# The rotation of queries and keys on GpSimd, issued behind VectorE's scalings in a hybrid attention kernel

## The chip, the cores and the metric

The kernel runs on one core of one Trainium2 chip. The metric is the device time of one execution in microseconds; lower is better. The core has five engines that run their own instruction queues and wait for one another through semaphores: TensorE (PE, with its weight loads as PEld), VectorE (DVE), ScalarE (ACT), GpSimd (POOL) and SyncE (SP, which only issues DMAs here).

## The reference

One layer of a decoder on a prompt of 2048 tokens and a sample batch of 8 x 8 tokens, all in float32, width 1024. One input projection feeds two groups of heads: group A, attention in a window of 128 positions with rotary positions, 8 query heads, 2 key heads and a learned sink per head; group B, gated linear attention. Both go through one output projection, then an MLP of width 4096. The change concerns group A alone:

```python
def rope(x, pos):
    ...
    x1, x2 = xf[..., :half], xf[..., half:]
    return jnp.concatenate([x1 * cos - x2 * sin, x2 * cos + x1 * sin], axis=-1).astype(x.dtype)

def sink_softmax(scores, mask, sink):
    scores = jnp.where(mask, scores, -jnp.inf)
    m = jnp.maximum(jnp.max(scores, axis=-1, keepdims=True), sink)
    p = jnp.exp(scores - m)
    return p / (jnp.sum(p, axis=-1, keepdims=True) + jnp.exp(sink - m))
```

In `swa_banded` each block of 128 queries sees its own and the previous block of keys: scores, `sink_softmax`, product with the values.

## The kernel before

The tokens are cut into 17 tiles: 16 of 128 prompt tokens and one of the 64 sample tokens. The program runs in stages: attention of group A (to about 345 us of the profile), then group B with the output projection, then the MLP. Within the attention stage one pass of the loop `for i in range(NB)` is a block: it computes attention for tile `i` and, between, the projection (`proj`), rotation and transposes for the tiles after it.

A block has four units, one per key head `r` and pair of query heads `jj`, in the order (0,0), (0,1), (1,0), (1,1). `unit` is a generator; each `next` issues one step: a copy of the sinks by GpSimd (L466), scores on TensorE (`sc`), masking and maximum on VectorE (into `s` and `m`), the exponential on ScalarE (which also sums into `den`), the division (a reciprocal of `den` and two scalings of `s` by it on VectorE), transposes on TensorE (`pT`), copies into a high part `ph` (ScalarE) and a low part `pl` (VectorE), products with the values on TensorE (`av`), and the sum `mo`. In loop step `u` the current unit `now` goes through mask to transposes, the unit `behind` finishes and the unit `ahead` starts. So each step `u` has one pair of scalings.

The order on TensorE, ScalarE and VectorE is written by hand: the wrapper `InOrder` (`te`, `ac`, `dv`) chains the instructions, and L141 is its line, so almost all of these engines' rows carry L141. GpSimd's order isn't chained; a scheduler places its instructions in the one queue by when it expects their inputs. The small jobs beside the units (`todo`) are placed by `A_PLAN`: a name, a step `u`, and a phase of it (A, X, B or C, in this order). `"turn": "1A"` is the rotation of tile `i + 1`.

`rotate` makes five GpSimd instructions: two products with the sine into `tb` (L385), one product with the cosine in place in `qk` (L391), and two additions into `rot` (L394, L400). TensorE transposes `rot` into `pq` and `pk` in step 2 of a block (`heads_T`), from which the operands `qh`, `ql`, `kh`, `kl` are made; GpSimd copies halves of the last two (L432, L436, L437, L443). In 8 blocks GpSimd also prepares weights of group B: two products with the gains (L271) and two subtractions (L273, `wg`), and in some blocks VectorE copies constants (L855).

Of the kernel before, what the change touches and what calls it, by code (L numbers as in the profile page):

```python
# [55 lines left out]
A_FILL = ((11, 2, 0), (10, 0, 2), (10, 0, 0), (12, 1, 0))  # L56
A_LEAD, A_SPLIT, A_PL_FIRST = 14, (2, 0, 0, 0), ()
A_PLAN = [(name, (int(at[0]), at[1])) for name, at in dict(
    first="1B", hi1="3B", x1="1B", lo1="0A", x0="0C", rest="3A", lo0="3A", junk="2A", turn="1A", rstd="1A", vl="3B"
).items()]  # L60
G_FIRST = (0, 1)
G_NEXT = (NB, *range(2, NB))
# [64 lines left out]
def f32(ap):  # L127
    return ap.bitcast(F32)
# [23 lines left out]
def hybrid_step_kernel(ctx: ExitStack, tc: tile.TileContext, I, O):  # L152
    nc = tc.nc
# [11 lines left out]
    def rows(i):  # L165
        return min(P, NTOK - i * P)
# [12 lines left out]
    def bank(shape, kind, name):  # L179

        return ps.tile(shape, F32, tag=kind, name=name, bufs=1 if kind in "de" else 2)
# [102 lines left out]
    sp = open_pool("a_s")  # L284
    sp.tile([P, 8], F32, name="a_edge")
    gxTs, ropes, xs_in, xTs, proj, qks, rots, heads, vals = {}, {}, {}, {}, {}, {}, {}, {}, {}
    stores = []

    stages = [("cache_k", 1), ("cache_v", 1), ("s", 3), ("ph", 2), ("pl", 2), ("qh", 2), ("ql", 2), ("mo", 2), ("tb", 1)]
    stages = [t for t in stages for _ in range(t[1])]  # L290
# [56 lines left out]
    def scaled(out, i, src):  # L347
        ac.activation(out, src, AF.Copy, scale=rstd_all[: rows(i), i : i + 1])

    def take_first(i):  # L350

        n = rows(i)
        qks[i] = sp.tile([P, 10, HD], F32, tag="qk", name=f"qk_{i}", bufs=2)
        scaled(qks[i].rearrange("p h d -> p (h d)")[:n, :A_N], i, proj.pop((i, 0))[:n, :A_N])

    def take_rest(i):

        n = rows(i)
        p_ = proj.pop((i, 1))
        w = 640 - A_N  # L360
        scaled(qks[i].rearrange("p h d -> p (h d)")[:n, A_N:640], i, p_[:n, :w])
        vps = p_[:n, w:A_N]
        if i == NB:
            vals[i] = vn = sp.tile([NS, P], F32, tag="vv", name="vn", bufs=4)
            scaled(vn, i, vps)
            return lambda: None
        vals[i] = vv = sp.tile([P, 2, 2, HD], F32R, tag="vv", name=f"vv_{i}", bufs=4)
        vh, vl = vv[:, :, 0, :], vv[:, :, 1, :]
        vps = vps.rearrange("p (r d) -> p r d", r=2)
        scaled(vh, i, vps)  # L370
        if i == NB - 1:
            vo = sp.tile([P, P], F32, tag="kc", name="vo", bufs=1)
            scaled(vo, i, p_[:n, w:A_N])
            stores.append((O["v_win_prompt"][0, 0].rearrange("w h d -> w (h d)"), vo))
        rs = rstd_all[:n, i : i + 1]
        return lambda: dv.scalar_tensor_tensor(vl, vps, rs, f32(vh), op0=ALU.mult, op1=ALU.subtract)

    def rotate(i, engine=nc.gpsimd):

        n = rows(i)  # L380
        qk, rope = qks.pop(i), ropes.pop(i)
        tb = sp.tile([P, 10, HD], F32, tag="tb", name=f"tb_{i}", bufs=1)
        for hf in range(2):
            sin = rope[:n, 1, hf * 32 : hf * 32 + 32].unsqueeze(1).to_broadcast([n, 10, 32])
            engine.tensor_tensor(  # L385
                tb[:n, :, hf * 32 : hf * 32 + 32], qk[:n, :, 32 - hf * 32 : 64 - hf * 32], sin, op=ALU.mult
            )
            if hf == 0:
                yield
        cos = rope[:n, 0, :].unsqueeze(1).to_broadcast([n, 10, HD])  # L390
        engine.tensor_tensor(qk[:n], qk[:n], cos, op=ALU.mult)  # L391
        yield
        rots[i] = rot = sp.tile([P, 5, 2, HD], F32, tag="rot", name=f"rot_{i}", bufs=1)
        engine.tensor_tensor(  # L394
            rot[:n, 0:4].rearrange("p j r d -> p r j d"),
            qk[:n, 0:8].rearrange("p (r j) d -> p r j d", r=2),
            tb[:n, 0:8].rearrange("p (r j) d -> p r j d", r=2),
            op=ALU.add,
        )
        engine.tensor_tensor(rot[:n, 4], qk[:n, 8:10], tb[:n, 8:10], op=ALU.add)  # L400
        yield
# [56 lines left out]
    def unit(i, r, jj, mo):  # L458

        nkt = min(i + 1, 2)  # L460
        nk = nkt * P
        rr = half_of[r]
        u_ = f"{i}_{r}_{jj}"
        h0 = r * 4 + jj * 2
        s = sp.tile([P, 2, nk + 1], F32, tag="s", name=f"s_{u_}", bufs=3)
        nc.gpsimd.tensor_copy(s[:, :, nk : nk + 1], sink[:, h0 : h0 + 2].unsqueeze(2))  # L466
        yield
        qs, ks, kl = heads[i]
        kh, kl = (t[:, r].rearrange("p a k -> p (a k)")[:, 2 * P - nk :] for t in (ks, kl))
        sc = bank([P, 2, nk], "b", f"sc_{u_}")  # L470
        for u in range(2):
            j = jj * 2 + u
            te.matmul(sc[:, u, :], qs[r][:, j, :], kh, start=True, stop=False)
            te.matmul(sc[:, u, :], qs[r][:, j, :], kl, start=False, stop=True)
        yield
        m = sp.tile([P, 2], F32, tag="m", name=f"m_{u_}", bufs=3)
        for u in range(2):
            dv.tensor_tensor_reduce(
                s[:, u, :nk], sc[:, u, :], amask[:, 2 * P - nk :], scale=1.0,
                scalar=sink[:, h0 + u : h0 + u + 1], op0=ALU.add, op1=ALU.min, accum_out=m[:, u : u + 1],  # L480
            )
        yield
        den = sp.tile([P, 2], F32, tag="den", name=f"den_{u_}", bufs=3)
        for u in range(2):
            ac.activation(
                s[:, u, :], s[:, u, :], AF.Exp, scale=-1.0, bias=m[:, u : u + 1], accum_out=den[:, u : u + 1]
            )
        yield
        dv.reciprocal(den, den)
        for u in range(2):  # L490
            dv.tensor_scalar(s[:, u, :nk], s[:, u, :nk], den[:, u : u + 1], None, op0=ALU.mult)
        yield
        pT = bank([P, nkt, 2, P], "c", f"pT_{u_}")
        for u in range(2):
            for kt in range(nkt):
                te.transpose(pT[:, kt, u, :], s[:, u, kt * P : (kt + 1) * P], ident)
        yield
        ph = sp.tile([P, nkt, 2 * P], F32R, tag="ph", name=f"ph_{u_}", bufs=2)
        pl = sp.tile([P, nkt, 2 * P], F32R, tag="pl", name=f"pl_{u_}", bufs=2)
        pf = pT.rearrange("p k u q -> p k (u q)")  # L500
        ac.activation(ph, pf, AF.Copy)
        yield
        dv.tensor_tensor(pl, pf, f32(ph), op=ALU.subtract)
        yield
        av = bank([P, 2 * P], "e", f"av_{u_}")
        vs = [vals[t] for t in range(i + 1 - nkt, i + 1)]
        both, hi, lo = ([v[:, r, u] for v in vs] for u in (slice(2), 0, 1))
        both = [v.rearrange("p u d -> p (u d)") for v in both]
        out = mo[rr, jj * 2 : jj * 2 + 2].rearrange("p j q -> p (j q)")
        if nkt == 1:  # L510
            te.matmul(av[:HD], hi[0], ph[:, 0], start=True, stop=False)
            te.matmul(av[:HD], hi[0], pl[:, 0], start=False, stop=False)
            te.matmul(av[:HD], lo[0], ph[:, 0], start=False, stop=True)
            yield
            ac.activation(out, av[:HD], AF.Copy)
        else:
            te.matmul(av, both[0], ph[:, 0], start=True, stop=False)
            for kt in range(2):
                te.matmul(av[:HD], hi[kt], pl[:, kt], start=False, stop=False)
            te.matmul(av, both[1], ph[:, 1], start=False, stop=True)  # L520
            yield
            rest = sp.tile([P, 2 * P], F32, tag="spc", name=f"rest_{u_}", bufs=2)
            ac.activation(rest[:HD], av[HD:], AF.Copy)
            yield
            dv.tensor_tensor(out, av[:HD], rest[:HD], op=ALU.add)
        if (r, jj) == (1, 1):
            stores.append((mix_d[i][:, 0:4, :], mo))
        yield
# [146 lines left out]
    def run(products, n=None):  # L675
        deque(products if n is None else islice(products, n), 0)

    def start():
# [58 lines left out]
        x2 = [*x_half(2, 0), *x_half(2, 1, "e")]  # L737
        take_first(0)
        rest = take_rest(0)
        x2[0]()  # L740
        turn = rotate(0, dv)
# [7 lines left out]
        x2[3]()  # L749
        take_first(1)  # L750
        rest = take_rest(1)
        rest()
        load_x(3)
# [39 lines left out]
    todo = {}  # L793
    for i in range(NB):
# [16 lines left out]
            gxTs[t] = load_T(t, [sp.tile([P, KT, P], F32R, tag=x, name=f"g{x}_{t}", bufs=2) for x in ("xh", "xl")])  # L811
            fill = chain(fill, projecting(t, gxTs[t], G_EARLY, ac))
        new = i + 3 < NTILE
        todo["turn"] = lambda: run(rotate(i + 1))
        if i + 2 < NTILE:
            todo["first"] = lambda: take_first(i + 2)
            todo["rest"] = lambda: todo.update(vl=take_rest(i + 2))
        if new:
            todo["junk"] = lambda: todo.update(rstd=x_norm(i + 3))
# [616 lines left out]
    turned, logs, seconds = {}, {}, []  # L1436
# [557 lines left out]
    turn = [0]  # L1994
# [121 lines left out]
    f, todo, slow, late = {}, deque(), deque(), DOWN_ORDER[-1]  # L2116
# [11 lines left out]
    for n, (sb, p, fc) in enumerate(units):  # L2128
# [3 lines left out]
        if n == len(units) - 4:  # L2132
# [5 lines left out]
            for j in range(4):  # L2138
                for m in range(4):
                    down_products(n + m, j)  # L2140
                i = 12 + j
# [89 lines left out]
```

## Time and profile before

| what | value |
|---|---|
| median of 3 runs | 2219.06 us (2218.36 to 2219.94) |
| profiled execution | 2217.48 us, of which its span is 2215.7 |
| granted TensorE clock | 0.999 of full speed |
| busy share: TensorE, VectorE, ScalarE, GpSimd | 98%, 71%, 55%, 11% |

The span goes from the first to the last instruction. A row of the timeline gives the start in us, the length in us, engine, line, operation, output and inputs, shapes, and how many equal instructions were merged; a bracket gives the idle time before it and who ended it. A row of the groups gives count, busy us, mean ns, and idle time before. A row of busy time by stretch gives the stretch, its length and for each engine the busy us and the instructions.

### The profile page before, as it was taken

How to read it: one execution, taken by the hardware profiler on the slowest of the kernel's cores; microseconds unless marked ns; L12 is line 12 of the kernel's file. 1: busy time of each engine (PE TensorE's matmuls, PEld its weight loads, DVE VectorE, ACT ScalarE, POOL GpSimd, SP SyncE). 2: the span in 40 equal slices, each digit the busy share in tenths (PEclk: the TensorE clock that was granted, in tenths of full speed). 3: DMA queues.
4: the chain of work that ended last, by engine and by line, in shares of the span. 5: the costliest groups of instructions: out<-in, count | busy, mean ns of one | idle time of the engine just before them, and what ended most of it. 6: DMA issues, size and time to landing. Idle time of an engine off the chain costs nothing.

```text
span 2215.7 us, 34304 instructions
## 1 busy us (share of the span) xinstructions
PE 2177.0 (98%) x11947; PEld 1865.5 (84%) x11947; DVE 1580.2 (71%) x3221; ACT 1222.5 (55%) x2549; POOL 250.6 (11%) x408
## 2 busy tenths in 40 slices
PE   8999999999999999999999999999999999999998
PEld 8888888899999888888888888888888888888886
DVE  5888877777778776687667788878545545855557
ACT  6777766555566443555555655555444444554445
POOL 3466522111111110000000000000000000000000
PEclk9999999999999999999999999999999999999999
DMA  7343322121113455765555766766765755866665
GB/s 240 120 139 138 108 95 89 57 73 62 53 49 120 157 192 195 261 224 185 200 189 189 273 208 212 242 233 221 230 207 178 232 175 184 292 232 217 219 196 202
DMA packets 229798, 392.64 MB, mean 177 GB/s; under 512 B 23379, under 2 KB 137882, under 8 KB 225642
## 3 DMA queue, kind: packets, MB, share of 16 engines
q1 hardware_dynamic: 229626, 390.47, 52.3%
q8 instruction: 94, 1.54, 0.3%
q14 instruction: 78, 0.64, 0.1%
HBM read 255.54 MB, written 135.86 MB: 177 GB/s over the span
## 4 chain that ended last, share of the span: by engine, by line
PE 83%; DVE 10%; ACT 5%; issue 2%; DMA 1%; POOL 0%; SPq 0%; DVEq 0%; ACTq 0%; POOLq 0%
PE dn L141 27%; PE gproj L141 10%; PE uc L141 7%; PE ua L141 7%; PE out L1337 6%; PE ud L141 4%; PE ub L141 4%; PE ue L141 4%; DVE s L141 2%; PE out L141 2%; PE sam L141 1%; PE proj L141 1%; PE gm L141 1%; PE dsam L141 1%; DVE pl L141 1%
## 5 line engine op out<-in xcount | busy, mean ns | idle before, releaser
L141 PE MATMUL dn<-ot,os 128*128 128x512 f32 x2688 | 621.2, 389 | 0.6 <-DVE ot L141 0.4
L141 PEld LDWEIGHTS dn<-ot,os 128*128 128x128 f32 x2688 | 504.2, 188 | 107.1 <-DVE ot L141 2.0
L141 DVE TENSOR_TENSOR os<-os 128x512 fp32r<-128x512 f32 x224 | 154.7, 690 | 228.1 <-ACT os L141 228.0
L141 ACT ACTIVATE os<-os 128x512 fp32r<-128x512 f32 x224 | 141.4, 631 | 278.1 <-DMA os<-s_d 219.5
L141 PE MATMUL gproj<-wg,gx 128*128 128x384 f32 (+1 forms) x1408 | 269.0, 343 | 0.0
L141 PEld LDWEIGHTS gproj<-wg,gx 128*128 128x128 f32 x1408 | 244.1, 188 | 5.0 <-issue 3.3
L141 ACT ACTIVATE st<-st 128x512 f32<-128x512 f32 x225 | 142.3, 633 | 137.4 <-DVE st L141 132.2
L141 PE MATMUL ua<-H,w 128*128 128x512 f32 x744 | 179.7, 390 | 0.3 <-DVE w L141 0.3
L141 PE MATMUL uc<-H,s 128*128 128x512 f32 x744 | 179.0, 389 | 0.0
L141 PEld LDWEIGHTS uc<-H,s 128*128 128x128 f32 x744 | 139.4, 188 | 29.2 <-DVE st L141 0.4
L141 PEld LDWEIGHTS ua<-H,w 128*128 128x128 f32 x744 | 138.5, 188 | 29.2 <-DVE w L141 1.1
L218 POOL TENSOR_TENSOR frs<-rs_v,half 128x1 f32<-128x1 f32 (+1 forms) x13 | 9.8, 751 | 1222.6 <-DVE rs_v L141 1222.6
L141 DVE TENSOR_TENSOR st<-st 128x512 f32<-128x512 f32 x160 | 110.4, 692 | 48.6 <-ACT st L141 45.4
L1337 PE MATMUL out<-wo,mt 128*128 128x512 f32 x608 | 141.5, 391 | 0.0
L1337 PEld LDWEIGHTS out<-wo,mt 128*128 128x128 f32 x608 | 113.2, 188 | 23.0
L141 ACT ACTIVATE s<-t 128x1024 fp32r<-128x1024 f32 x62 | 65.7, 1059 | 62.7 <-PE ue L141 24.6
L141 DVE TENSOR_TENSOR s<-t,s 128x1024 fp32r<-128x1024 f32 x62 | 75.9, 1225 | 33.9 <-ACT s L141 31.0
L141 DVE TENSOR_TENSOR ot<-ot 128x512 fp32r<-128x512 f32 x128 | 88.2, 689 | 10.9 <-ACT ot L141 9.8
L141 PE MATMUL proj<-wa_hi,xh 128*128 128x384 f32 (+1 forms) x272 | 95.2, 353 | 0.9 <-ACT wa_hi L141 0.6
L141 PE MATMUL proj<-wa_lo,xh 128*128 128x384 f32 (+1 forms) x272 | 93.9, 349 | 0.0
L141 PE MATMUL proj<-wa_hi,xl 128*128 128x384 f32 (+1 forms) x272 | 92.7, 345 | 0.0
L141 ACT ACTIVATE ot<-ot 128x512 fp32r<-128x512 f32 x128 | 80.8, 631 | 17.5 <-DMA ot<-t_d 13.5
(424 smaller groups left out, 4053.2 us busy)
## 6 DMA issues: line engine op xcount, KB each, us to landing
os<-s_d SPq DMA_DIRECT2D x224, 256.0 KB, 2.8
s_d<-st SPq DMA_DIRECT2D x31, 1792.0 KB, 8.9
raw<-in_w_up SPq DMA_DIRECT2D x64, 512.0 KB, 6.8
ot<-t_d SPq DMA_DIRECT2D x128, 256.0 KB, 3.2
rt<-in_w_down SPq DMA_DIRECT2D x96, 256.0 KB, 3.0
t<-in_w_down SPq DMA_DIRECT2D x64, 256.0 KB, 3.3
t_d<-t SPq DMA_DIRECT2D x32, 512.0 KB, 7.0
gx<-xt_d SPq DMA_DIRECT2D x28, 512.0 KB, 5.3
```

The source lines that it names most:

```text
L141: ins = call(*a, **k)
L218: nc.gpsimd.tensor_tensor(out, v[:n], e, op=ALU.pow)
L1337: te.matmul(p_, x, w[:, cc], start=k + u == 0, stop=k == KT - 1 and u == len(products) - 1)
```

## The change

The rotation is issued one to two steps of a unit earlier in the hand-written plan, in two halves, each of which is tied behind a small GpSimd memset. In phase C of step 3 of block `i` the products for tile `i + 2` are issued (`begin`), in phase C of step 0 of the next block the additions (`turned`). Ahead of each half stands a memset that writes zeros into `den` of the unit scaled last; VectorE's scalings read this `den`, so the memset waits for them, and `tc.issue_after` puts the half behind the memset in GpSimd's queue. The `den` that it overwrites is not read again. The rotation of tile 1 stays at step 1, phase A of the first block, undivided; the rotation of tile 0 is VectorE's and stays.

```diff
 A_PLAN = [(name, (int(at[0]), at[1])) for name, at in dict(
-    first="1B", hi1="3B", x1="1B", lo1="0A", x0="0C", rest="3A", lo0="3A", junk="2A", turn="1A", rstd="1A", vl="3B"
+    first="1B", hi1="3B", x1="1B", lo1="0A", x0="0C", rest="3A", lo0="3A", junk="2A", turn="1A", rstd="1A", vl="3B", begin="3C", turned="0C"
 ).items()]
...
+    def behind_scaling():
+
+        if not scaled_by:
+            return nullcontext()
+        return tc.issue_after(nc.gpsimd.memset(scaled_by[-1], 0.0).ins)
...
             dv.tensor_scalar(s[:, u, :nk], s[:, u, :nk], den[:, u : u + 1], None, op0=ALU.mult)
+        scaled_by.append(den)
...
-        todo["turn"] = lambda: run(rotate(i + 1))
+        if i == 0:
+            todo["turn"] = lambda: run(rotate(1))
+
+        def begin_turn(turn):
+            with behind_scaling():
+                run(turn, 2)
+            todo["turned"] = lambda: end_turn(turn)
+
+        def end_turn(turn):
+            with behind_scaling():
+                run(turn)
+
         if i + 2 < NTILE:
             todo["first"] = lambda: take_first(i + 2)
+            todo["begin"] = lambda: begin_turn(rotate(i + 2))
```

The order of instructions on TensorE, VectorE and ScalarE is the same as before, row for row. GpSimd's queue before, around the rotation of tile 11 (`tb_3176`), from the copy of step 3 to the weight work of the next block's step 0; the numbers behind names count buffers, and `s_1_0`, `s_1_1` are the score tiles of units of the next block:

```order
L443 CAST kl_3014<-kl_3014 64x128
L385 TENSOR_TENSOR tb_3176<-qk_2967,rope_2312 128x10x32 x2
L391 TENSOR_TENSOR qk_2967<-qk_2967,rope_2312 128x640
L394 TENSOR_TENSOR rot_3180<-qk_2967,tb_3176 128x2x4x64
L400 TENSOR_TENSOR rot_3180<-qk_2967,tb_3176 128x128
L466 COPY s_1_0_3110<-sink 128x2
L443 CAST kl_3014<-kl_3014 64x128
L437 CAST kl_3274<-kl_3014 128x2x128
L466 COPY s_1_1_3186<-sink 128x2
L273 TENSOR_TENSOR wg_1_188<-wg_raw_2901,wg_0_187 128x384
L273 TENSOR_TENSOR wg_1_188<-wg_raw_2903,wg_0_187 128x384
```

The same place of GpSimd's queue now (the lines of the file have moved: L391 is the sine product, L397 the cosine product, L400 and L406 the additions, L472 the copy of the sinks, L443 and L449 the copies of `kl`):

```order
L449 CAST kl_3032<-kl_3032 64x128
L382 MEMSET den_1_1_3061 128x2
L391 TENSOR_TENSOR tb_3112<-qk_2985,rope_2329 128x10x32 x2
L397 TENSOR_TENSOR qk_2985<-qk_2985,rope_2329 128x640
L472 COPY s_1_0_3133<-sink 128x2
L449 CAST kl_3032<-kl_3032 64x128
L443 CAST kl_3294<-kl_3032 128x2x128
L382 MEMSET den_0_0_3127 128x2
L400 TENSOR_TENSOR rot_3193<-qk_2985,tb_3112 128x2x4x64
L406 TENSOR_TENSOR rot_3193<-qk_2985,tb_3112 128x128
L472 COPY s_1_1_3206<-sink 128x2
L273 TENSOR_TENSOR wg_1_188<-wg_raw_2922,wg_0_187 128x384
```

The products keep their place behind the copy of `kl` but have a memset on `den_1_1` (the last unit of the block) before them; the additions have moved behind the sink copy and two copies of `kl`, with a memset on `den_0_0` (the first unit of the next block) before them, directly ahead of the sink copy and the weight work. Before, the five instructions stood together.

SyncE's queue before, where the stores of the last rotated keys stand:

```order
L329 DMA out_v_win_prompt<-vo 128x128
L329 DMA out_k_win_prompt<-rot_4181 128x128
L329 DMA mix_d_77<-mo_3754 128x512
L592 DMA gxh_4361<-xt_d_82 128x1024
L592 DMA gxl_4362<-xt_d_82 128x1024
L329 DMA new_v<-vn 64x128
L329 DMA new_k<-rot_4432 64x128
L893 DMA out_v_win_sample<-new_v 8x1024
L893 DMA out_k_win_sample<-new_k 8x1024
L329 DMA mix_d_78<-mo_4000 128x512
L239 DMA wg_raw_4416<-in_w_in 128x384
```

SyncE's queue now at this place:

```order
L329 DMA out_v_win_prompt<-vo 128x128
L329 DMA mix_d_77<-mo_3778 128x512
L329 DMA out_k_win_prompt<-rot_4202 128x128
L599 DMA gxh_4394<-xt_d_82 128x1024
L599 DMA gxl_4395<-xt_d_82 128x1024
L329 DMA new_v<-vn 64x128
L912 DMA out_v_win_sample<-new_v 8x1024
L329 DMA mix_d_78<-mo_4026 128x512
L239 DMA wg_raw_4449<-in_w_in 128x384
L329 DMA new_k<-rot_4455 64x128
L912 DMA out_k_win_sample<-new_k 8x1024
```

The store of the prompt's keys has moved behind one store of `mix_d`, that of the sample's keys behind another and one weight load, and the copy out of `new_k` with it.

More of the change, by code (lines that the diff above doesn't have):

```diff
@@ L286, in hybrid_step_kernel @@
     gxTs, ropes, xs_in, xTs, proj, qks, rots, heads, vals = {}, {}, {}, {}, {}, {}, {}, {}, {}
-    stores = []
+    stores, scaled_by = [], []
     stages = [("cache_k", 1), ("cache_v", 1), ("s", 3), ("ph", 2), ("pl", 2), ("qh", 2), ("ql", 2), ("mo", 2), ("tb", 1)]
```

## The prediction

> **What bounds the kernel now.** I read the page's head first, then busy time by stretch, then the chain of waits in one block of the attention stage, then the rows of VectorE (DVE), GpSimd (POOL) and the weight loads of TensorE (PEld) in that block.
>
> ```profile
> span 2215.7 us, 34304 instructions
> PE 2177.0 (98%) x11947; PEld 1865.5 (84%) x11947; DVE 1580.2 (71%) x3221; ACT 1222.5 (55%) x2549; POOL 250.6 (11%) x408
> core 0: us, PE busy (x) PEld busy (x) DVE busy (x) ACT busy (x) POOL busy (x), PEclk, DMA share, GB/s
> 48.00:294.00 246.00, 230.22 (x1520) 210.32 (x1518) 215.26 (x621) 185.51 (x504) 142.26 (x254) 1.00 0.36 125
> 345.00:2215.00 1870.00, 1856.28 (x9835) 1571.81 (x9833) 1304.80 (x2422) 979.46 (x1903) 90.07 (x118) 1.00 0.55 184
> ```
>
> From 345 us on TensorE is busy 1856 of 1870 us: what the attention stage saves shifts all of this forward and is kept. In the attention blocks (48 to 294 us) TensorE is idle for 15.8 us and VectorE is busy for 215 of 246. The next rows are the chain of waits in the block that ends near 216 us: start, length, what.
>
> ```profile
> 207.70 1.51 DVE s L141 x2
> ...
> 216.17 0.07 DVE rs_v L141
> 216.24 0.55 PE av L141 x3
> ```
>
> The chain stays on VectorE from 207.70 to 216.24 (the rows left out are all VectorE's or its issue). `DVE s L141 x2` at 207.70 is the pair of scalings s * den of unit (1,1), the block's last. I call it the closing pair; the next block's pair of unit (0,0), at 212.73, is the opening pair; unit (0,1), at 216.59, the second pair.
>
> ```profile
> 206.47 0.27 DVE L141 TENSOR_TENSOR kl<-pk,kh 64x128 fp32r<-64x128 f32 x1
> 207.70 1.51 DVE L141 TENSOR_SCALAR s<-s,den 128x256 f32<-128x256 f32 x2
> 212.73 0.86 DVE L141 TENSOR_SCALAR s<-s,den 128x256 f32<-128x256 f32 x2
> 216.59 0.62 DVE L141 TENSOR_SCALAR s<-s,den 128x256 f32<-128x256 f32 x2
> 225.17 1.51 DVE L141 TENSOR_SCALAR s<-s,den 128x256 f32<-128x256 f32 x2
> 206.88 0.29 POOL L443 CAST kl<-kl 64x128 fp32r<-64x128 f32 x1 [0.61 <-DVE kl L141]
> 207.32 1.74 POOL L385 TENSOR_TENSOR tb<-qk,rope 128x320 f32<-128x320 f32 x2 [0.15 <-ACT qk L141]
> 209.13 1.57 POOL L391 TENSOR_TENSOR qk<-qk,rope 128x640 f32<-128x640 f32 x1
> 210.78 1.29 POOL L394 TENSOR_TENSOR rot<-qk,tb 128x512 f32<-128x512 f32 x1
> 212.03 0.47 POOL L400 TENSOR_TENSOR rot<-qk,tb 128x128 f32<-128x128 f32 x1
> 212.69 0.29 POOL L443 CAST kl<-kl 64x128 fp32r<-64x128 f32 x1
> 213.04 0.40 POOL L437 CAST kl<-kl 128x256 fp32r<-128x256 f32 x1
> 214.41 1.99 POOL L273 TENSOR_TENSOR wg<-wg_raw,wg 128x384 fp32r<-128x384 f32 x2
> L855 DVE COPY c<-c_raw 64x8 f32<-64x8 f32 x1 | 0.8, 769 | 0.0
> ```
>
> The same pair takes 0.62 us with no large GpSimd work beside it and 1.51 beside the two `tb` products. It ends at 209.21, which is 0.15 after `tb` (207.32 + 1.74 = 209.06). The opening pair ends at 213.59, again 0.15 after L437 (213.44). So such a VectorE operation waits until GpSimd's current one has ended and finishes 0.15 later; its own start is not lost. A copy of 8 elements a row takes 769 ns in the last row, from the same cause.
>
> ```profile
> 208.46 0.20 PEld L141 LDWEIGHTS pT<-ident,s 128*128 128x128 f32 x2 [0.35 <-ACT ql L141]
> 209.32 0.20 PEld L141 LDWEIGHTS pT<-ident,s 128*128 128x128 f32 x2 [0.67 <-issue]
> 216.22 0.19 PEld L141 LDWEIGHTS av<-pl,vv 128*64 128x64 f32 x2 [0.46 <-DVE rs_v L141]
> 217.25 0.19 PEld L141 LDWEIGHTS sc<-kh,ql 128*128 128x128 f32 x1
> 220.09 0.25 PEld L141 LDWEIGHTS av<-pl,vv 128*64 128x64 f32 x2
> 220.45 0.46 PEld L141 LDWEIGHTS pq<-ident,rot 128*128 128x128 f32 x4
> ```
>
> TensorE waits 0.35 + 0.67 us at the transposes that read the closing pair, then 0.46 at `av` for the end of the VectorE chain. (The names in the brackets are those of work long done; the release fits the pair's two halves.)
>
> **The change, part by part.**
>
> *Closing pairs.* The rotation's first half (`tb` twice, `qk`) now waits for the pair's end, so the pair should take 0.62. Which pairs are hit:
>
> ```profile
> L385 POOL TENSOR_TENSOR tb<-qk,rope 128x320 f32<-128x320 f32 x30 | 25.9, 885 | 2.9 <-ACT qk L141 1.0 <-DMA wg_raw<-in_w_in 0.9
> 48.10 1.45 DVE L141 TENSOR_SCALAR s<-s,den 128x128 f32<-128x128 f32 x2
> 64.84 1.80 DVE L141 TENSOR_SCALAR s<-s,den 128x256 f32<-128x256 f32 x2
> 293.66 1.45 DVE L141 TENSOR_SCALAR s<-s,den 128x256 f32<-128x256 f32 x2
> L141 DVE TENSOR_SCALAR s<-s,den x128: 281/354/958, 37.8 to 310.1; 128x256 f32<-128x256 f32 x120, 128x128 f32<-128x128 f32 x8
> ```
>
> There are 30 `tb` of 128 rows and 2 of 64, so 16 rotations. That of tile 1 keeps its place; 15 move. Of their pairs the first loses 0.97 (1.45 less 0.48, two narrow scalings that overlap by 0.08 as the wide ones do), the second 1.18 (1.80 less 0.62), the last 0.83, and the 12 between 0.89 each as at 207.70: 0.97 + 1.18 + 0.83 + 10.68 = 13.66 us. This lies on the path: VectorE has no gap from the pair to `av`, and TensorE's waits of 1.02 have room for 0.89.
>
> *Opening pairs.* GpSimd starts 0.14 after VectorE's end (L443 at 206.88 after `kl` at 206.74). The memset of 128x2 is not in the trace; between these rows it takes the small one's 0.10 (nearest in size), at most 0.31:
>
> ```profile
> L2219 POOL MEMSET const-float32-1.0<- 128x1 f32 x1 | 0.1, 98 | 0.0
> L1106 POOL MEMSET after<- 128x256 f32 x16 | 5.0, 311 | 136.2 <-ACT dec L1047 135.1 <-issue 1.1
> L273 POOL TENSOR_TENSOR wg<-wg_raw,wg x16: 1010/1029/1055, 106.8 to 232.9; 128x400 fp32r<-128x400 f32 x8, 128x384 fp32r<-128x384 f32 x8
> 217.30 0.42 DVE L141 TENSOR_TENSOR mo<-av,rest 64x256 f32<-64x256 f32 x1
> 217.93 0.69 DVE L141 TENSOR_TENSOR xl<-xT,xh 128x512 fp32r<-128x512 f32 x1 [0.21 <-ACT xh L141]
> 52.23 0.87 DVE L141 TENSOR_SCALAR s<-s,den 128x256 f32<-128x256 f32 x2
> 298.37 0.65 DVE L141 TENSOR_SCALAR s<-s,den 128x256 f32<-128x256 f32 x2
> ```
>
> So `qk` ends 0.14 + 0.10 + 1.74 + 0.07 + 1.57 = 3.62 us after the closing pair. VectorE begins the opening pair 3.52 after it (209.21 to 212.73, without a gap). The overlap is 0.10, and 0.10 + 0.15 is less than one scaling's 0.35: nothing lost on the first scaling. L443, behind `qk`, falls on the second; today L443 and L437 cost 0.24 there. I count no change; free, it would give 10 such blocks 2.4 us more; with the memset at 0.31, 0.2 less in 15 blocks, 3 us. [...]
>
> *Second pairs.* The additions `rot` now wait for the opening pair, and L273 stands behind them. Eight blocks have two L273. There GpSimd needs, from the opening pair's end, 0.14 + 0.10 + 1.72 (`rot`, 210.78 to 212.50) + 0.19 (the copy of the sinks, which today fills 212.50 to 212.69) + 1.99 = 4.14 us; the first L273 ends at 3.1. VectorE starts the second pair at 3.00 (213.59 to 216.59) and would end it at 3.62. The first scaling passes, the second waits for 4.14 + 0.15: 0.67 late. Today L273 ends at 216.40, before the pair. Behind it VectorE has 0.09 of idle time before `mo` and 0.21 before `xl`, which absorb 0.30; TensorE's next `av` at 220.09 shows no wait, and I give it no slack: 0.37 reach TensorE. 8 x 0.37 = 3.0 us lost; at least 0, at most 5.4.
>
> *Edges.* In the first block VectorE needs only 2.68 between the pairs (49.55 to 52.23), less than 3.62, so `qk` runs 0.94 into the opening pair: it loses about 0.6 where it loses 0.25 now. The last has 3.26 (295.11 to 298.37) and loses 0.2. Together 0.6 us.
>
> *Hidden.* The 30 memsets are 3 us on an engine that is busy 11%. Behind a waiting memset stand the sink copies, L443 and L437. TensorE reads L443's half at 217.25, today 4.3 us after it is written, and transposes `rot` at 220.45, 7.9 us after; `rot` comes about 3 us later against the rest: both covered; without that cover TensorE would wait for GpSimd there. SyncE's stores of the last keys move one and three issues back and wait for a `rot` that is ready by then, with the late weight loads behind the second: 0.
>
> Sum: 13.66 - 3.0 - 0.6 = 10.1 us. The profiled execution took 2217.48 (span 2215.7 and 1.8 around it), so it would take 2207.4. It is 1.6 under the median of the runs, 2219.06; against that median I forecast 2209.0.
>
> **Rivals.**
> - *The stall moves.* L273 costs its whole 5.4 us and GpSimd starts 0.2 later each time: 13.66 - 5.4 - 0.6 - 3 = 4.7, 2214.4. For it: the margin is 0.1 us at both places. Against: VectorE's idle time behind the second pair.
> - *No change.* The pair gets short but TensorE, once it no longer waits there, waits as long for something else, 2219. For it: TensorE has other waits in the block (0.46 at `av`). Against: those waits also end with the same VectorE chain, so they move with it.
> - *Slower.* GpSimd gets going late behind the memset. From 0.1 us on, each 0.1 adds 0.1 to 15 opening pairs. At 1.0 us the gain of 0.89 is gone; at 1.3 the loss is 15 x 0.3 = 4.7 plus 3.0 at L273: 2227. Against: 0.14 and 0.15 are the waits on other engines that GpSimd shows above.
> - *All of it.* Opening pairs come free and L273 is absorbed: 13.66 + 2.4 = 16 us, 2203.
>
> **How the numbers follow.** The likeliest case (a gain of 7 to 14 us, 2205 to 2212) gets 0.72, the moved stall 0.12, all of it 0.06, no change 0.06, slower 0.04. Runs of before spread by 1.6 us, so 0.2% (4.4 us) is about what a measurement of this kernel tells from no change. Faster: 0.72 + 0.12 + 0.06 = 0.90; same 0.06; slower 0.04. The range takes in both bounds of the opening pairs and of L273: 2203.5 to 2214.5.
>
> **What would show it.** Right: closing pairs at 0.62 with `tb` starting 0.2 behind them; TensorE's waits at `pT` under 0.2; blocks without L273 near 16.6 us from closing pair to closing pair (17.47 now, 207.70 to 225.17 in the views above); second pairs of about 1.2 in eight blocks. Wrong: opening pairs over 1.2 us, or blocks of 17.4 with a new wait of TensorE. The forecast falls if memset and wait together take over 0.5 us.

## Result and the profile after

The changed kernel takes 2207.26 us (median of 4 runs, 2206.19 to 2207.87) against 2218.85 (4 runs, 2218.36 to 2219.94): a ratio of 0.9945, 95% interval 0.9933 to 0.9958. The forecast for the median was 2209.0; the profiled execution took 2206.19 us where the forecast for it was 2207.4.

The head of the page and the busy time in the same stretch as before (the columns are those of the prediction's table):

```profile
span 2204.4 us, 34353 instructions
PE 2176.2 (99%) x11947; PEld 1867.0 (85%) x11947; DVE 1572.8 (71%) x3221; ACT 1221.9 (55%) x2549; POOL 252.2 (11%) x438
```

```profile
48.00:294.00 246.00, 239.86 (x1597) 221.09 (x1596) 219.48 (x651) 195.21 (x529) 148.49 (x291) 1.00 0.37 127
```

TensorE's wait for the scaled weights in that stretch (total us, times, longest), after and then before:

```profile
PE pT L141 <- DVE s L141: 0.6, 2, 0.3
```

```profile
PE pT L141 <- DVE s L141: 7.4, 17, 0.5
```

TensorE's work over the whole span is the same to 1 us; its idle time in the 246 us fell from 15.8 to 6.1, and its wait for the scaled weights from 7.4 to 0.6. The block that the prediction showed, now on VectorE and then on GpSimd (L391 is the sine product, L397 the cosine product, L400 and L406 the additions):

```profile
198.46 0.62 DVE L141 TENSOR_SCALAR s<-s,den 128x256 f32<-128x256 f32 x2
202.59 0.67 DVE L141 TENSOR_SCALAR s<-s,den 128x256 f32<-128x256 f32 x2
206.26 1.50 DVE L141 TENSOR_SCALAR s<-s,den 128x256 f32<-128x256 f32 x2
210.87 0.84 DVE L141 TENSOR_SCALAR s<-s,den 128x256 f32<-128x256 f32 x2
215.22 0.62 DVE L141 TENSOR_SCALAR s<-s,den 128x256 f32<-128x256 f32 x2
```

```profile
199.22 0.10 POOL L382 MEMSET den<- 128x2 f32 x1 [1.29 <-ACT ql L141]
199.28 1.71 POOL L391 TENSOR_TENSOR tb<-qk,rope 128x320 f32<-128x320 f32 x2
201.07 1.56 POOL L397 TENSOR_TENSOR qk<-qk,rope 128x640 f32<-128x640 f32 x1
...
203.51 0.10 POOL L382 MEMSET den<- 128x2 f32 x1
203.57 1.29 POOL L400 TENSOR_TENSOR rot<-qk,tb 128x512 f32<-128x512 f32 x1
204.82 0.46 POOL L406 TENSOR_TENSOR rot<-qk,tb 128x128 f32<-128x128 f32 x1
205.23 0.19 POOL L472 COPY s<-sink 128x2 f32<-128x2 f32 x1
205.37 1.98 POOL L273 TENSOR_TENSOR wg<-wg_raw,wg 128x384 fp32r<-128x384 f32 x2
...
210.47 0.83 POOL L271 TENSOR_TENSOR wg_raw<-wg_raw,gcol 128x384 f32<-128x384 f32 x1 [0.71 <-DMA wg_raw<-in_w_in]
```

The closing pair (198.46, 215.22) is back at 0.62 us, and `tb` starts 0.20 behind its end. The opening pair (202.59) has 0.67. The second pair (206.26) now has L273 beside it and takes 1.50; the third (210.87) meets L271, whose DMA lands later because it is issued only when L273 has read the raw weights (at 207.38, just behind L273's end at 207.35). From closing pair to closing pair it is 16.76 us here; blocks without L273 take 16.40 (17.47 before).

One row serves as the yardstick for every kernel below: all scalings s * den, with the start of the first and of the last. The time between them I call the stage. After:

```profile
L141 DVE TENSOR_SCALAR s<-s,den x128: 281/353/1240, 37.1 to 296.8; 128x256 f32<-128x256 f32 x120, 128x128 f32<-128x128 f32 x8
```

The stage takes 296.8 - 37.1 = 259.7 us; by the same row of before, which the prediction shows, it took 310.1 - 37.8 = 272.3. It is 12.6 us shorter; the second profile of the changed kernel (37.3 to 297.0) has 259.7 too.

| kernel | median us (runs) | ratio to before, 95% | stage us |
|---|---|---|---|
| changed | 2207.26 (4) | 0.9945, 0.9933 to 0.9958 | 259.7 |
| changed, again (e9_again) | 2207.70 (5) | 0.9948, 0.9935 to 0.9960 | 259.7 |
| e1_no_tie | 2219.23 (10) | 0.9996, 0.9986 to 1.0005 | 272.1 |
| e10_one_tie | 2215.46 (11) | 0.9982, 0.9973 to 0.9991 | 269.4 |
| e2_unsplit | 2217.34 (10) | 0.9984, 0.9975 to 0.9993 | 267.5 |
| e4_late | 2214.13 (8) | 0.9975, 0.9964 to 0.9985 | 266.5 |
| e3_odd | 2222.77 (10) | 1.0011, 1.0002 to 1.0021 | 272.7 |
| e6_scalare (last scaling on ScalarE) | 2208.34 (4) | 0.9951, 0.9936 to 0.9965 | 260.6 |
| e5_l273 | 2207.79 (4) | 0.9943, 0.9928 to 0.9958 | 260.2 |
| e7_warm | 2208.43 (4) | 0.9950, 0.9934 to 0.9967 | 259.8 |
| e8_copies / e11_best | 2202.37 (4) / 2200.33 (4) | 0.9921, 0.9906 to 0.9936 / 0.9915, 0.9901 to 0.9928 | 256.0 / 255.2 |
| e12_last | 2200.44 (5) | 0.9916, 0.9902 to 0.9929 | 254.7 |

### The profile page after: what moved, and what is told of

Same layout as the page of the kernel before. It is cut to its first block, busy times and chain, and to the rows that moved or that the text cites. A ratio compares the mean times of both kernels' runs of the same rounds, so it can differ in the third digit from the quotient of the medians.

```text
span 2204.4 us, 34353 instructions
## 1 busy us (share of the span) xinstructions
PE 2176.2 (99%) x11947; PEld 1867.0 (85%) x11947; DVE 1572.8 (71%) x3221; ACT 1221.9 (55%) x2549; POOL 252.2 (11%) x438
## 4 chain that ended last, share of the span: by engine, by line
PE 85%; DVE 6%; ACT 5%; issue 2%; DMA 1%; POOL 1%; SPq 0%; DVEq 0%; ACTq 0%; POOLq 0%
PE dn L141 27%; PE gproj L141 11%; PE uc L141 7%; PE ua L141 7%; PE out L1356 6%; PE ud L141 4%; PE ub L141 4%; PE ue L141 4%; PE proj L141 3%; PE out L141 2%; PE sam L141 1%; PE gm L141 1%; PE dsam L141 1%; ACT s L141 1%; DVE s L141 1%
## 5 line engine op out<-in xcount | busy, mean ns | idle before, releaser
L141 ACT ACTIVATE ot<-ot 128x512 fp32r<-128x512 f32 x128 | 80.7, 631 | 16.6 <-DMA ot<-t_d 11.3
## 6 DMA issues: line engine op xcount, KB each, us to landing
os<-s_d SPq DMA_DIRECT2D x224, 256.0 KB, 2.8
ot<-t_d SPq DMA_DIRECT2D x128, 256.0 KB, 3.2
rt<-in_w_down SPq DMA_DIRECT2D x96, 256.0 KB, 3.0
t<-in_w_down SPq DMA_DIRECT2D x64, 256.0 KB, 3.3
```

What stands on the lines that cost most here:

```text
L141: ins = call(*a, **k)
```

## The experiments

**Is it the wait, or the new places in the program?** The changed order, without the memsets that tie it:

```
 def behind_scaling():
-    if not scaled_by: return nullcontext()
-    return tc.issue_after(nc.gpsimd.memset(scaled_by[-1], 0.0).ins)
+    return nullcontext()
```

> The changed kernel without its two memsets: the rotation is planned at the new places, but nothing makes it wait for a scaling, and it stands in GpSimd's queue where it stood before. Theory A (the gain is the closing pair of scalings no longer blocked by the products on GpSimd): closing pairs back at 1.5 us, the time back at 2219 (within 2). Rival B (the earlier place in the plan is what helps): 2207 to 2210.

```profile
207.71 1.51 DVE L141 TENSOR_SCALAR s<-s,den 128x256 f32<-128x256 f32 x2
212.73 0.87 DVE L141 TENSOR_SCALAR s<-s,den 128x256 f32<-128x256 f32 x2
```

These are the closing and the opening pair of the same block, as in the kernel before, and the stage takes 272.1 us: the other places alone give nothing. The wait makes the gain.

**Is the second tie needed?** The changed kernel with the additions left untied:

```
 def end_turn(turn):
-    with behind_scaling():
-        run(turn)
+    run(turn)
```

> The changed kernel with the rotation still split in two at the same places of the program, but without the second memset: the additions rot are no longer tied behind the opening pair, and GpSimd may start them as soon as the products are done. Theory A (the second tie is needed: without it rot stands behind qk and the sink copy and falls on the opening pair): opening pairs from 0.67-0.86 to 1.5-1.8, closing pairs still 0.62, second pairs beside L273 shorter, since L273 comes earlier against them (0.62 to 0.9); 15 x 0.9 lost and about 3 us given back: 2215 to 2219. Theory B (GpSimd is busy with the products and the copies until the opening pair is over anyhow, so the second tie holds nothing back): opening pairs under 0.9, time within 1 us of the changed kernel or 1 us less, 2205.5 to 2208.

```profile
205.32 0.62 DVE L141 TENSOR_SCALAR s<-s,den 128x256 f32<-128x256 f32 x2
209.46 1.64 DVE L141 TENSOR_SCALAR s<-s,den 128x256 f32<-128x256 f32 x2
214.10 0.62 DVE L141 TENSOR_SCALAR s<-s,den 128x256 f32<-128x256 f32 x2
```

```profile
209.58 1.37 POOL L400 TENSOR_TENSOR rot<-qk,tb 128x512 f32<-128x512 f32 x1
```

The closing pair stays short, the stall of 1.0 us goes to the opening pair, beside `rot`, and the second pair goes free. The stage gains only 2.9 of the 12.6 us, as theory A said: the second tie is needed. The second tie without the first was not tried.

**The whole rotation behind the closing pair**, not split:

```
-    run(turn, 2)
-todo["turned"] = lambda: end_turn(turn)
+    run(turn)
```

> The changed kernel with all five instructions of the rotation behind the closing pair and no second tie. Theory A: closing pairs stay at 0.62, but the additions (1.3 us) now run into the opening pair, which rises from about 0.7 to 1.7, while the second pairs fall back to 0.62 to 0.8: nearly the whole gain of 0.89 per block is lost, 2215 to 2219. Rival B (only the place of the products matters, the split is decoration): opening pairs about as now, 2207 (within 2).

```profile
204.17 0.62 DVE L141 TENSOR_SCALAR s<-s,den 128x256 f32<-128x256 f32 x2
208.31 1.64 DVE L141 TENSOR_SCALAR s<-s,den 128x256 f32<-128x256 f32 x2
```

The same picture, and theory A holds again: 4.8 us of the stage gained, blocks of 17.37. The rotation needs 5 us of GpSimd and VectorE leaves 3.5 between two pairs; in one piece it does not fit.

**How much room is there?** A second memset, of a scratch tile, behind each of the thirty:

```
-return tc.issue_after(nc.gpsimd.memset(scaled_by[-1], 0.0).ins)
+tied = nc.gpsimd.memset(scaled_by[-1], 0.0)
+with tc.issue_after(tied.ins):
+    wide = nc.gpsimd.memset(scratch, 0.0)
+return tc.issue_after(wide.ins)
```

> The changed kernel with a second GpSimd memset (a scratch tile of 128x512) behind each of the 30 memsets on den, so that GpSimd starts each half of the rotation later by that memset. From the memset of 128x256 (311 ns) and the one of 128x1 (98 ns) I estimate 0.52 us for it. Theory A (the margins of GpSimd at the opening and the second pair are about 0.1 us, so whatever delays GpSimd lands on VectorE): closing pairs stay at 0.62, opening pairs go from 0.67-0.86 to 1.2-1.4, second pairs in the eight blocks with L273 from 1.4-1.5 to 1.8-2.0; 15 x 0.5 + 8 x 0.45 = 11 us lost, nearly the whole gain: 2215 to 2219. Theory B (GpSimd has room there, and the memset and the wait could have been far slower without harm): opening pairs under 0.9 and a time within 2 us of the changed kernel, 2206 to 2209.

```profile
207.76 1.00 DVE L141 TENSOR_SCALAR s<-s,den 128x256 f32<-128x256 f32 x2
211.76 1.76 DVE L141 TENSOR_SCALAR s<-s,den 128x256 f32<-128x256 f32 x2
```

The extra memset takes 0.52 us, as estimated. A start that much later costs 0.33 at the opening pair (1.00 against 0.67) and 0.26 at the second, and the stage loses 6.8 us: 0.3 in most blocks without L273, 0.6 to 0.75 in those with it. Theory A had the direction and overstated the size: 2214.13 instead of 2215 to 2219. The prediction's slower rival had the mechanism right too (0.4 was its price for an opening pair 0.5 later), but its point of decision (1.0 us late) was not tried.

**Who is stopped?** The kernel before, with ScalarE doing the closing pair:

```
+if (r, jj) == (1, 1):
+    ac.activation(s[:, u, :nk], s[:, u, :nk], AF.Copy, scale=den[:, u : u + 1])
+else:
     dv.tensor_scalar(s[:, u, :nk], s[:, u, :nk], den[:, u : u + 1], None, op0=ALU.mult)
```

> The kernel before, with the closing pair's two scalings done by ScalarE (a copy with scale den) instead of VectorE; GpSimd's rotation stays beside them as before. Theory A (only VectorE is stopped by GpSimd's work in SBUF): each scaling takes about 0.46 us on ScalarE, as its copy of 128x256 does, the pair about 0.85 whatever GpSimd does; blocks without L273 fall from 17.47 to about 16.5-16.9, time 2205 to 2212. Theory B (GpSimd's work stops whoever reads or writes SBUF there): the pair takes 1.5 or more on ScalarE too, blocks 17.4 or longer, time 2218 or more. A third way: the scalings are quick but ScalarE's copies behind them (rest, ql) come 0.85 later and VectorE or TensorE waits for them: blocks 17.2-17.8 with a pair of 0.85.

One pair on ScalarE with the two `tb` beside it, and then all 32 scalings in one row (shortest, median, longest in ns):

```profile
215.97 1.69 POOL L385 TENSOR_TENSOR tb<-qk,rope 128x320 f32<-128x320 f32 x2 [0.15 <-ACT qk L141]
216.39 0.90 ACT L141 ACTIVATE s<-s,den 128x256 f32<-128x256 f32 x2
```

```profile
L141 ACT ACTIVATE s<-s,den x32: 389/497/503, 48.7 to 298.6; 128x256 f32<-128x256 f32 x30, 128x128 f32<-128x128 f32 x2
```

None is stretched, with `tb` beside it or without: the pair takes 0.90 on ScalarE where it took 1.51 on VectorE, and none of the 32 scalings takes over 503 ns. Most blocks without constant copies take 16.60, the stage is 0.9 us longer than that of the changed kernel and the time 1.1, with no wait added to GpSimd at all. Theory A held.

**Does the stall hang on an even count of columns?** The kernel before, with 257 columns in the closing pair (the last one, the sink's, is read by nothing afterwards). I supposed that an odd count makes a difference:

```
+wide = nk + ((r, jj) == (1, 1))
-dv.tensor_scalar(s[:, u, :nk], s[:, u, :nk], ...)
+dv.tensor_scalar(s[:, u, :wide], s[:, u, :wide], ...)
```

> The kernel before, where only the closing pair of each block scales 257 columns instead of 256 (129 instead of 128 in the first block; the extra column is not read again). [...]

```profile
208.37 1.44 DVE L141 TENSOR_SCALAR s<-s,den 128x257 f32<-128x257 f32 x2
310.43 0.62 DVE L141 TENSOR_SCALAR s<-s,den 128x257 f32<-128x257 f32 x2
```

A miss: with no GpSimd work beside it (310.43) the odd pair takes 0.62 like the even one, so nothing shows that the odd width changed how the operation runs. My estimate was 0.9 for the odd pair beside the products; it takes 1.44 in the block shown, where the even one of the kernel before takes 1.51. The 0.11% above before came from the later stages (the stage is within 0.4 us of before). The profiled execution, the slowest of the ten, has a mean granted clock of 0.998, like that of the changed kernel; why the ten runs as a whole are longer I do not know.

**The stall at the second pair.** The changed kernel with L273 tied behind the second pair:

```
 # split_gw
-nc.gpsimd.tensor_tensor(lo, raw, f32(hi), op=ALU.subtract)
+subs.append(lambda: nc.gpsimd.tensor_tensor(lo, raw, f32(hi), op=ALU.subtract))
 # main loop, ahead of do(u, "C")
+if u == 1 and subs:
+    with behind_scaling():
+        while subs: subs.pop(0)()
```

> The changed kernel with the two subtractions of the weight work (L273) also tied behind a scaling, that of the second pair. Theory A: in the eight blocks with L273 the second pairs fall from 1.4 to 0.62; what they cost TensorE now is the difference between blocks with and without L273 (16.77 against 16.40 in the plain ones, more in the three that also copy constants), so 3 to 5 us less: 2203 (within 2). The third pairs, hit by L271 now, may move either way by 0.3. Rival D (the stall of the second pair is absorbed by VectorE's idle time): 2207 (within 1).

All second pairs are at 0.62, and the four blocks that have L273 but no constant copies (the fifth and the tenth to twelfth) fall from 16.77 to 16.39-16.47, about the 0.37 expected; yet the stage is 0.5 longer. The other four blocks with L273 (the sixth to ninth) have VectorE's seven copies of constants (L874, L855 in the kernel before), of which four now meet L273 and take 0.92 to 1.06 us where the changed kernel has 0.19 to 0.27:

```profile
120.58 0.62 DVE L141 TENSOR_SCALAR s<-s,den 128x256 f32<-128x256 f32 x2
...
122.53 0.99 DVE L874 CAST c_suf<-c_raw 128x128 fp32r<-128x128 f32 x1
...
125.35 0.98 DVE L141 TENSOR_SCALAR s<-s,den 128x256 f32<-128x256 f32 x2
```

```profile
121.38 2.05 POOL L273 TENSOR_TENSOR wg<-wg_raw,wg 128x400 fp32r<-128x400 f32 x2
```

**The copies out of the way**: the kernel of the last experiment with the constant copies in blocks 13 to 16, and then the same kernel beside the changed one on one chip:

```
-if i > 4 and u % 2 and copies:
+if i > 11 and u in (1, 2) and copies:
```

> The changed kernel with L273 behind the second pair (as in the experiment on L273) and VectorE's seven constant copies moved from the sixth to ninth blocks into blocks 13 to 16, where no L273 runs. Theory A (what that experiment gave back was the constant copies meeting L273): second pairs 0.62 in all blocks, third pairs 0.62, the blocks with L273 all at 16.4-16.5 us where the changed kernel has 16.77-17.56, together about 4.4 us, less up to 1.5 us for the copies at their new place: 2203 to 2205. Rival (the weights come later and something behind the attention stage waits for them, or the copies meet other GpSimd work): no gain against the changed kernel, 2206 to 2209.

> The changed kernel once more, beside the two kernels of this set on the same chip, for a direct comparison. All theories: 2206 to 2209.

> The kernel with L273 behind the second pair and the constant copies in blocks 13 to 16 once more, beside the changed kernel on the same chip. Both theories: the gain of its first timing repeats, 3.5 to 6 us under the changed kernel, 2201.5 to 2203.5; if that was the chip's scatter, within 2 us of the changed kernel.

The cast of `c_suf` in the kernel so made, and its yardstick:

```profile
L874 DVE CAST c_suf<-c_raw x1: 217/217/217, 237.7 to 237.7; 128x128 fp32r<-128x128 f32 x1
```

```profile
L141 DVE TENSOR_SCALAR s<-s,den x128: 279/352/1071, 37.7 to 292.9; 128x256 f32<-128x256 f32 x120, 128x128 f32<-128x128 f32 x8
```

It takes 217 ns there instead of the 986 beside L273, the blocks with L273 take 16.39 to 16.46, and the stage is 4.5 us shorter than that of the changed kernel. On one chip the medians are 2200.33 (2200.24 to 2200.82) and 2207.70 (2206.32 to 2209.24): the largest gain of the study, and more than the 3.5 to 6 expected. Of these 7.4 us the stage holds 4.5, just above theory A's 2.9 to 4.4: it is confirmed there. The rest lies in later stages; the changed kernel's five runs alone spread over 2.9 us, and whether that rest belongs to the change is open.

**The last block.** Its yardstick had got worse: from the fifteenth closing pair to the sixteenth 16.69 us after, 16.16 before. In the changed kernel VectorE's part of the late weights, behind the opening pair, runs beside the additions:

```profile
283.74 1.05 DVE L141 TENSOR_SCALAR s<-s,den 128x256 f32<-128x256 f32 x2
285.27 1.52 DVE L141 SCALAR_TENSOR_TENSOR wg<-wg_raw,gcol,wg 128x384 fp32r<-128x384 f32 x1
289.84 0.62 DVE L141 SCALAR_TENSOR_TENSOR wg<-wg_raw,gcol,wg 128x384 fp32r<-128x384 f32 x1
```

```profile
285.08 1.28 POOL L400 TENSOR_TENSOR rot<-qk,tb 64x512 f32<-64x512 f32 x1
```

```profile
288.25 0.45 PE L141 MATMUL av<-pl,vv 128*64 128x256 f32 x2 [1.02 <-DVE pl L141]
```

The operation on `wg` takes 1.52 us beside `rot` and 0.62 without, and TensorE waits 1.02 for the chain behind it. It ends 0.42 behind the end of that addition, where a stopped scaling ends 0.15 behind.

The best kernel, with the last additions untied:

```
-    with behind_scaling():
+    with behind_scaling() if i < NB - 1 else nullcontext():
         run(turn)
```

> The best kernel so far (L273 behind the second pair, the constant copies in blocks 13 to 16), with the second tie left out for the last rotation alone, in block 16. There VectorE's wg<-wg_raw,gcol,wg of 128x384, behind the opening pair, takes 1.52 us beside the tied additions rot where it takes 0.62 without. Theory E (those 0.9 us are a stall of this operation by rot, and reach the end of the stage): from the fifteenth to the sixteenth closing pair 15.9 us instead of 16.88, the first scaling to the last pair of the attention stage 254.0 instead of 255.0, time about 1 us less than its 2200.3: 2198.5 to 2200. Rival (the stall only moves to the opening pair, which then takes 1.6 or more, or the later stages take the gain back): 16.6 to 17 us, time 2200 to 2202.

```profile
278.97 0.76 DVE L141 TENSOR_SCALAR s<-s,den 128x256 f32<-128x256 f32 x2
280.21 1.07 DVE L141 SCALAR_TENSOR_TENSOR wg<-wg_raw,gcol,wg 128x384 fp32r<-128x384 f32 x1
```

That block falls from 16.88 to 16.01, about as theory E said, though `wg` still meets `rot` and takes 1.07. The stage falls by 0.5 and not by the 1.0 expected, since other blocks are a little longer in this execution. The time, 2200.44, does not show it: half a microsecond is less than these kernels' runs scatter.

**A dip of TensorE's clock** (below) was tried with ten transposes put into the wait ahead of it:

```
+for _ in range(10 if i == 2 else 0):
+    te.transpose(tT[:, 0, :], ident, ident)
 for g in range(2):
     te.transpose(tT[:, g, :], parts[0][:, g * P : (g + 1) * P], ident)
```

> The changed kernel with ten extra transposes of the identity (about 1.3 us of TensorE work, overwritten afterwards) in the one wait of 1.62 us at 372 us, ahead of the transposes of zt. Theory C (the granted clock falls to 0.5 for 3.4 us at 374.59 because TensorE idles through half of the 3.4 us before): no such stretch there in the profile, 11 gproj matmuls behind it in about 2.3-2.6 us instead of 3.69, time 1.0 to 1.5 us less: 2205.5 to 2206.5 on the scale of the changed kernel's 2207.3. Theory D (the stretch comes from elsewhere, or at random): it is still there at 374-378, or the time is the same within 0.5 us.

```profile
374.13 1.31 PE L141 MATMUL tT<-ident 128*128 128x128 f32 x10 [1.62 <-DVE zt L993]
376.39 2.28 PE L141 MATMUL gproj<-wg,gx 128*128 128x400 f32 x11
```

The extra transposes waited as long as the others and ran behind the wait, not in it. The matmuls took 2.28 us and no dip came, but since the idle time was not filled, that is no proof for theory C, and the second profile of the changed kernel has a mean granted clock of 0.999 too, against 0.998 in its first. The median is 1.2 us above the changed kernel's, within what these runs spread (3.5 us).

## Why the prediction came out right, step by step

- *Closing pairs.* Forecast 13.66 us. Summed over the closing pairs, what lies above 0.62 (0.485 for the narrow ones) went from 13.6 us to 0. That this shortens the blocks shows in four that have no L273 (the fourth and the thirteenth to fifteenth): 1.0 to 1.1 us less, of which 0.88 to 0.90 are the closing pair ahead of the block and the rest its opening pair.
- *Opening pairs.* Forecast 0, with a gain of 2.4 as one end. Without the first and the last, their stall went from 2.4 to 1.3 us: ten blocks gained 1.7 and three, whose opening pairs had been free, lost 0.6. So 1.1 were gained, about the middle between the two. `tb` started 0.20 after the pair instead of my 0.24, since the memset overlaps what follows it (its record ends at 199.32, that of `tb` begins at 199.28); the copies behind `qk` still cost 0.05 to 0.24.
- *Second pairs.* 0.37 per block was forecast and 0.37 came (16.77 against 16.40), partly by luck. I let the first scaling pass and stopped the second; in fact the first one, which comes 0.1 before the first L273 ends, was stopped by both L273: 1240 ns, the longest in the yardstick row. It ended 0.15 after the second L273, and the other scaling followed with most of its own length, so the pair lost 0.88, not 0.67. VectorE's idle time behind it absorbed 0.5, not 0.3.
- *Third pairs.* Not foreseen: L271 made seven of them 0.2 to 0.6 longer, 2.8 us in all. It cost nothing: blocks with a third pair of 0.62 and of 1.08 both take 16.77.
- *Constant copies.* Not priced, though the prediction shows one of them as an example of the stall. Their seven durations add up to 4.0 us in the kernel before and 2.3 in the changed one. The four blocks that hold them gained 3.8 us together, the four other blocks with L273 2.8, although the opening pairs of the first four got 0.4 longer together and those of the others 0.7 shorter. If L273 costs the same 0.37 in all eight, the copies gave about 2.0 us.
- *Edges.* The opening pair behind the first closing pair is stopped for 0.71 us (forecast 0.6), but that cost nothing: from that closing pair to the next it is 0.96 shorter, all that the closing pair itself gave. The last block's lost 0.43 (0.2), and 0.9 more at `wg` (1.52 us beside `rot`, 0.62 without), which the forecast left out.
- *Signs.* Closing pairs at 0.62 and `tb` 0.2 behind them came as named. Blocks without L273 take 16.40 and not 16.6, since the opening pairs got shorter too; second pairs in the eight blocks take 1.4 to 1.5 and not 1.2; TensorE's waits at `pT` are nearly gone, but the two left reach 0.3 us, and its weight loads' 0.5, where under 0.2 was named.

On the stage: 13.6 + 1.1 + 2.0 - 3.0 - 0.4 - 0.9 = 12.4 of the 12.6 us measured. The forecast for the stage was 10.1. Between the two profiled executions the span differs by 11.3: 1.3 us of the stage's gain are lost again later, where the clock dip described last costs 1.4. So the mechanism and the largest term were right, but that the time came within 2 us of the forecast is in part luck: 3.1 us of gains that were not in the sum (opening pairs and copies) met losses that were not in it either (`wg` and the later stages).

The stopped scalings do not need their full 0.35 us after GpSimd's instruction. In the changed kernel 26 scalings are more than 0.05 us longer than the unhindered ones, and each of them ends 0.15 behind an instruction of GpSimd; in the kernel before there are 48, of which 46 end 0.15 to 0.16 behind one and two narrow ones 0.08 and 0.09.

## What to carry to other kernels

Where VectorE and GpSimd work side by side, look for VectorE rows whose longest duration is far over the median (958 ns against 354 for the scalings of the kernel before), and at what GpSimd runs beside them; then tie GpSimd's work to start behind the VectorE operation, in pieces that fit the gap before the next one, each piece with its own tie. Every piece moved falls on something: list all of VectorE's operations at the new place that got longer beside GpSimd (here scalings, up to 1240 ns against 353; the copy of 64x8, 769 ns before and 348 after; the cast of `c_suf`, 986 against 217; the operation on `wg`, 1.52 us against 0.62), since moving the weights' subtraction and the copies as well shortened the stage by another 4.5 us. Moving the stopped operation to ScalarE, which was busy for 55% of the span, was worth nearly as much without any wait (11.7 us of the stage against 12.6).

## What was not expected of the hardware

TensorE's granted clock falls to one half for 3.4 us in the profiled execution of the changed kernel. It is shown in two stretches (the third number from the end is the clock), and eleven matmuls in the second stretch, after and then before:

```profile
371.00:374.60 3.60, 1.92 (x32) 1.41 (x30) 3.36 (x12) 1.92 (x6) 0.71 (x1) 1.00 0.53 185
374.60:378.00 3.40, 3.40 (x15) 3.13 (x10) 2.86 (x11) 1.55 (x6) 0.00 (x0) 0.50 0.00 0
```

```profile
374.87 3.69 PE L141 MATMUL gproj<-wg,gx 128*128 128x400 f32 x11
```

```profile
388.05 2.28 PE L141 MATMUL gproj<-wg,gx 128*128 128x400 f32 x11
```

The eleven matmuls take 1.4 us longer. By the clock record of this execution the dip lasts 3.413 us, from 374.59 to 378.01, and begins 361.81 us after the clock first rose (at 12.78), which is 106 times that length. In the 3.413 us before it TensorE was busy for 51%. Cut into stretches of this length from the same point, the execution has one of 61% (398.49 to 401.90) that no dip followed. In the kernel before, where the clock first rose at 13.65 and fell to one half only at the end, from 2211.84, the lowest of these stretches has 66%. From 345 to 420 us the mean granted clock is 0.98 in the profiled executions of e4_late, e6_scalare and e8_copies, as in this one, and 1.00 in those of before and e7_warm. Why the dip came here, behind a wait of 1.62 us (373.59), and none in the kernel before behind the same wait of 1.63 (386.87), is open.
